# One layer of a hybrid encoder: small steps and small tiles moved at the start, at the first scores and at the end

## The chip, the cores and the metric

The kernel runs on one core of a Trainium2 chip. The metric is the device time of one execution in microseconds (us); where several runs of a kernel are known, their median stands for it.

A core has a matrix engine (TensorE, PE in the profile; the load of its weights has a line of its own, PEld), three engines for elementwise work (VectorE = DVE, ScalarE = ACT, GpSimd = POOL), and SyncE (SP), which in this kernel only issues DMA transfers. Each engine runs its own instructions in the order in which the program issues them, and waits on semaphores for the others. Tiles lie in SBUF (128 partitions wide); results of TensorE lie in PSUM banks of 128 x 512 float32.

## What is computed

One layer on x of 256 tokens by 2048 features, in float32:

```
h = rmsnorm(x) * g1
q, k, v, u = split(h @ w_in)           # 12 query heads, 4 key and value heads of 128; u has 512 columns
a = rmsnorm(window_attention(q, k, v)) # |t - s| <= 128, a slope per head on |t - s|, a sink logit per head
f = rmsnorm(per group of 128 channels: real(fft2(u)) @ w_fourier)
x = x + concat(a, f) @ w_out
h = rmsnorm(x) * g2
gate, val = split(h @ w_up)            # 5504 columns each
x = x + (gelu(conv3(gate)) * val) @ w_down
y = rmsnorm(x) * gf
```

An rmsnorm multiplies each token's row by (mean of its squares + 1e-6)^-0.5, one scale per token, and by a gain per feature. Because the scale belongs to a token, it can be applied behind a matrix product; the kernel does so.

## The kernel before

**Units.** All weights together are some 180 MB, and every weight is used once. They come as units of 128 x 2048 float32 (1 MB): 0 to 3 for u, 4 to 7 for v, 8 to 23 for the query and key heads in the order k0, q0, q1, q2, k1, ..., 24 to 39 for w_out, and then the feed-forward part. TensorE multiplies float32 in a shortened form, so each operand is cut in two: `hi`, a cast copy, and `lo`, the rest. A unit is loaded by a DMA issued on SP into one of three `raw` buffers (L121), ACT makes `hi` from it (L143), DVE makes `lo` = raw - hi (L144), and the load of unit i + 3 is issued right behind the split of unit i (L146), since it takes that unit's buffer. The product is hi x hi + hi x lo + lo x hi. For u, v, w_out and w_down the weights are the moving operand, 512 columns wide, three matmuls for each block of 128 features and each half of the tokens (`moving_weights`, L269 to L271). For q, k and w_up the weights stand still (`still_weights`, L280 and L281).

**The order of steps.** Nothing is scheduled by a planner: the order on each engine is that of the code. `unit(i, work)` (L312) does, for every unit from 4 on up to the end of w_out: the steps hung `before` i, the matmuls of unit i, the steps hung `beside` i, then `step(i)`, which splits unit i + 2, then the steps hung `behind` i. A step hung on a unit puts its matmuls ahead of that unit's on TensorE, or its copies ahead of the split of unit i + 2 (beside) or behind it (behind) on ACT, DVE and POOL. Within one list, the order is that of registration.

**The start.** SP issues the pieces of the transposed input xT (`load_x`; eight tiles of 256 KB, the first in two halves) and of units 0, 1 (quarters) and 2 (halves) in an order written out by hand (L175 to L198). For each of the 16 feature blocks k, `split_scaled` (L230) makes the parts of x times g1, ACT and DVE split a piece of the weights, and six matmuls add to the two u banks `ps_u` (loop at L324). At k = 0 the first piece of the weights is split ahead of the scaled x; at other k behind it.

**Scales of the tokens.** The untransposed x comes as four tiles `xs` of 128 x 2 x 512, issued after the loads of units 4 and 5 (L202 to L207). `token_sums(c)` (L352) takes two sums of squares on ACT for a tile; `token_scales` (L356) adds them up on DVE, raises to the power -0.5 on POOL, copies the result to `r1` on DVE and derives three small tiles for the scores from it. The sums of tiles 0 and 1 stand behind unit 4, those of 2 and 3 and the scales behind unit 5. With `r1`, `rows_out` (L365) cuts u into `u_hi` and `u_lo` beside unit 6, and v beside unit 8.

**The Fourier part.** A small product of the channel matrix with w_fourier (`fourier_weights`, ahead of unit 6) is copied out beside unit 6, and so is the split of the position matrix, `pos_hi` on ACT and `pos_lo` on DVE (`fourier_positions`, L421). Ahead of unit 7, `fourier_rows` multiplies u by the positions (24 matmuls into four `ps_f`, L449). Ahead of units 8 and 9 stand two channel groups each (`fourier_channels`, L468), and beside them `fourier_channels_out` (L473): a copy on ACT, three joins on DVE, the split into a `cat` tile and a square on ACT and DVE, and an addition of squares on POOL (L402). The sum of the squares over the features, `ps_totf`, stands ahead of unit 11. `spread` (L251) turns `r1` from a column into a row across all partitions, with two diagonals on DVE, two matmuls and a copy, all ahead of unit 8.

**The scores.** q and k heads leave PSUM beside the unit behind theirs (`qk_out`, `qk_parts`); the scores of a head stand ahead of the second unit behind its own, that is those of q0 (unit 9) ahead of unit 11. ACT's last step before them is `qT` (L232).

**The end.** The last group of w_down is computed block by block, (column block c, token half b) in the order (0,0), (0,1), (1,0), (1,1), (2,0), (3,0), (2,1), (3,1), the last in two halves p of 256 columns. `last_post` (L808) adds a block to `xs` on DVE (L811), takes its sum of squares on ACT (L797) and multiplies it by the last gain on POOL, unless c is 3 (L814). `finish(b, n)` (L818) adds up n sums, makes the scale (DVE L240, POOL L242) and writes the four outputs y of a token half: two on ACT (L833), one on DVE with two inputs (L827), one on DVE with one (L831). `finish(0, 4)` stands at (3,0), ahead of the additions of block (2,1); `finish(1, 5)` comes last.

**Pools.** `base` holds what lives throughout, `ph` (named "pa") what lives to the end of w_out, `wp` the raw, hi and lo buffers; `wp`'s addresses follow those of `base`.

The functions that the change touches, and their callers:

Of the kernel before, what the change touches and what calls it, by code (L numbers as in the profile page):

```python
# [20 lines left out]
GQA = 3  # L21
NG = 4
AW = NH * HD
FW = NG * P
DFF = 5504
NF = DFF // P
EPS = 1e-6
# [29 lines left out]
def block_kernel(  # L57
# [17 lines left out]
    nc = tc.nc  # L75
# [10 lines left out]
    def bank(pool, name):  # L86
        return pool.tile([P, 512], F32, tag=pool.name, name=name)
# [79 lines left out]
    def load_x(c, o=0, n=512):  # L167
        nc.sync.dma_start(xTc[c][:, o : o + n], xT[:, c * 512 + o : c * 512 + o + n])
# [6 lines left out]
    first = load(0, 4)  # L175
# [4 lines left out]
    next(first)  # L180
    load_x(1)
    next(first)
    load_x(2)
    next(first)
    load_x(3)
    second = load(1, 4)
    next(second)
    load_x(4)
    next(second)
    next(second)  # L190
    load_x(5)
    next(second)
    for _ in second:
        pass
    load_x(6)
    for _ in load(2, 2):
        pass
    load_x(7)  # L198

    def load_more(i):  # L200

# [25 lines left out]
    def vcol(o, n=1):  # L227
        return vec[:, o : o + n]
# [5 lines left out]
            dst[:, S : 2 * S], src, g, f32(dst[:, 0:S]), ALU.mult, ALU.subtract  # L234
        )

    def rstd_of(ssq, width, name, n=2):

        var = base.tile([P, n], F32, tag="var" + name, name="var" + name)
        nc.vector.tensor_scalar(var, ssq, 1.0 / width, EPS, ALU.mult, ALU.add)  # L240
        r = base.tile([P, n], F32, tag="rstd" + name, name="rstd" + name)
        nc.gpsimd.tensor_tensor(r, var, half_pow[:, 0:n], ALU.pow)  # L242
        return r

# [3 lines left out]
            junk, t[:, b, :], AF.Square, accum_out=parts[:, b, c : c + 1]  # L248
        )

    def spread(r, dst, name):  # L251

        ps = bank(dn, "ps_spread" + name)
        for b in range(2):
            dg = base.tile([P, P], F32, tag=f"diag{b}", name=f"diag{name}{b}")
            nc.vector.tensor_scalar(dg, ident, r[:, b : b + 1], None, ALU.mult)
            nc.tensor.matmul(
                ps[:, b * P : (b + 1) * P], ones, dg, start=True, stop=True
            )
        nc.vector.tensor_copy(dst, ps[:, :S])  # L260


    def moving_weights(hi, lo, n, kk, act, b, ps, first, last, q0=0):
# [41 lines left out]
    def at(when, i, f, *a):  # L305
        when.setdefault(i, []).append((f, a))
# [17 lines left out]
    for k in range(NK):  # L324
        c, q = k // 4, k % 4
        if q == 0:
            parts = split_parts(c, 4 if c < 2 else 2)
        if k == 0:
            next(parts)
        split_scaled(hk(k), xTc[k // 2][:, (k % 2) * S : (k % 2 + 1) * S], vcol(V_G1 + k))  # L330
        if k:
            next(parts, None)
        hi, lo = halves[c]
        for b in range(2):
            moving_weights(
                hi, lo, 512, [k], hk, b, ps_u[b], k == 0, k == NK - 1, q0=q
            )
        if q == 3:
            for _ in parts:
                pass  # L340
            del halves[c]
# [1 line left out]
    split(5)  # L343

    ssq1 = base.tile([P, 2, 4], F32, tag="ssq1", name="ssq1")
    r1 = base.tile([P, 2], F32, tag="r1", name="r1")
    rq_neg = base.tile([P, 2], F32, tag="rq_neg", name="rq_neg")
    rq_pos = base.tile([P, 2], F32, tag="rq_pos", name="rq_pos")
    rq_inv = base.tile([P, 2], F32, tag="rq_inv", name="rq_inv")
    sink_neg = base.tile([P, NH], F32, tag="sink_neg", name="sink_neg")  # L350

    def token_sums(c):  # L352
        for b in range(2):
# [38 lines left out]
    def feature_out(ps, slot, g, sq, first):  # L392

        t = cat_pool.tile([P, 512], F32R, tag="cat", name=f"cat{slot}")
        split_scaled(t, ps, g)
        cat[slot] = t
        if first:
            nc.scalar.activation(sq, ps, AF.Square)
        else:
            one = ph.tile([P, S], F32, tag="sq1", name=f"sq{slot}", bufs=1)  # L400
            nc.scalar.activation(one, ps, AF.Square)
            nc.gpsimd.tensor_tensor(sq, sq, one, ALU.add)  # L402
# [67 lines left out]
                us[g][:, o : o + n], start=True, stop=True,  # L470
            )

    def fourier_channels_out(g):  # L473
        h = ph.tile([P, S], F32, tag="tmp", name=f"yh{g}", bufs=2)
        nc.scalar.activation(h, held.pop(("y", g))[:, 0:S], AF.Copy)
        y = ph.tile([P, S], F32, tag="add", name=f"y{g}", bufs=2)
        nc.vector.tensor_tensor(y[:, 1:H], h[:, 1:H], h[:, H + 1 : S], ALU.add)
        nc.vector.tensor_tensor(
            y[:, H + 1 : S], h[:, H - 1 : 0 : -1], h[:, S - 1 : H : -1], ALU.subtract
        )  # L480
        nc.vector.tensor_copy(y[:, 0 : H + 1 : H], h[:, 0 : H + 1 : H])
        feature_out(y, NH + g, vcol(V_GF + g), sq_f, g == 0)

    def token_scales_across():
        spread(r1, r1b, "1")

    def distances():

# [2 lines left out]
            nc.vector.tensor_scalar(rel[:, s], rel[:, s], rq_inv[:, b : b + 1], None, ALU.mult)  # L491
        nc.vector.tensor_scalar(sink_neg, vcol(V_SINK, NH), -1.0, None, ALU.mult)

    at(before, 6, fourier_weights)
# [12 lines left out]


    ps_v = [bank(mm, f"ps_v{b}") for b in range(2)]
# [124 lines left out]
    for i in range(N_QK, N_OUT + 8):  # L634
# [18 lines left out]
        if 2 in heads:  # L653
            at(beside, i, scores_out, heads[2])
            at(behind, i, exps, heads[2])

    for n, (kind, h) in enumerate(QK_ORDER):

        def work(hi, lo):
            ps = st["ps", kind, h] = bank(mm, f"ps_{kind}{h}")  # L660
            still_weights(hi, lo, ps, range(NK))

        unit(N_QK + n, work)
# [151 lines left out]
                xb, xb, gfb[:, c * 512 + o : c * 512 + o + n], ALU.mult  # L815
            )

    def finish(b, n):  # L818
        tot = base.tile([P, 1], F32, tag=f"tot3{b}", name=f"tot3{b}")
        nc.vector.tensor_reduce(tot, ssq3[:, b, 0:n], mybir.AxisListType.X, ALU.add)  # L820
        r = rstd_of(tot, D, f"3{b}", 1)
        y = [
            fp.tile([P, 512], F32, tag="act", name=f"y{b}{c}", bufs=12) for c in range(4)
        ]
        for c in (0, 3, 1, 2):
            if c == 3:
                nc.vector.scalar_tensor_tensor(  # L827
                    y[c], xs[c][:, b, :], r, gfb[:, 1536:2048], ALU.mult, ALU.mult
                )
            elif c == 2:  # L830
                nc.vector.tensor_scalar(y[c], xs[c][:, b, :], r, None, ALU.mult)  # L831
            else:
                nc.scalar.activation(y[c], xs[c][:, b, :], AF.Copy, scale=r)  # L833
            nc.sync.dma_start(
                out[b * P : (b + 1) * P, c * 512 : (c + 1) * 512], y[c]
            )
# [164 lines left out]
```

## Time and profile before

| | us |
|---|---|
| runs | 998.82, 999.02, 1000.75; median 999.02 |
| profiled execution | 999.48 |
| its span (first to last instruction) | 997.6 |
| TensorE busy | 982.8 (99%) |
| VectorE busy | 696.9 (70%) |
| ScalarE busy | 466.6 (47%) |
| GpSimd busy | 23.5 (2%) |
| DMA, mean over the span | 187 GB/s |

The profile has several views. The first page's head gives the busy time of each engine. *Busy time by stretch* gives, for a window A:B in us from the span's start, its length, then the busy time of PE, PEld, DVE, ACT and POOL with their counts, the clock granted to TensorE, and the mean busy share of the 16 DMA engines with the GB/s. *The timeline* gives a start, a duration, the engine, the line, the operation, the tile written and those read, and in brackets the idle time of the engine before it with what ended it. *TensorE's waits* gives, for a tile and the producer waited for, the total, the count and the longest. *The chain of waits* is the chain of work that ended last, in order of time: start, duration, engine, tile and line. Matmuls are pipelined: a row's duration goes from its start to its end, and the next one can start before.

### The profile page before, as it was taken

Reading aid. Unit: us, or ns where it says so; the run is one execution under the profiler, and the core shown is the slowest. Engines: PE = TensorE matmul, PEld = TensorE weight load, DVE = VectorE, ACT = ScalarE, POOL = GpSimd, SP = SyncE. Lnnn points to the kernel's source line nnn. Section 1 sums busy time; section 2 is a strip of 40 time slices with the busy share of each in tenths; the row PEclk is TensorE's granted clock in tenths of the full one; section 3 lists DMA queues with packets and bytes.
Section 4 is the critical chain, followed back from the end, with each engine's and each line's share of the span. In section 5 each row is a group of like instructions: output and inputs, shape, how many; then the busy total and the mean of one; then the engine's idle time right before and its main releaser. Section 6 shows DMA issues by size and latency. Waiting matters only on the chain.

```text
span 997.6 us, 12850 instructions
## 1 busy us (share of the span) xinstructions
PE 982.8 (99%) x5185; PEld 839.6 (84%) x5185; DVE 696.9 (70%) x934; ACT 466.6 (47%) x587; POOL 23.5 (2%) x35
## 2 busy tenths in 40 slices
PE   8999999999999999999999999999999999999996
PEld 6788888888888888888888888888888888888885
DVE  6567877666687776767767767767676777676764
ACT  6646666554554434444434434344344343443434
POOL 0000000000000000000000000000000000000003
PEclk9999999999999999999999999999999999999998
DMA  9834434445645555555555555555645555555532
GB/s 335 339 127 169 165 132 169 135 169 208 239 156 191 187 193 193 188 194 187 174 206 171 210 172 201 177 193 185 209 170 195 185 180 200 173 205 188 194 127 85
DMA packets 30091, 186.42 MB, mean 187 GB/s; under 512 B 3408, under 2 KB 3920, under 8 KB 9040
## 3 DMA queue, kind: packets, MB, share of 16 engines
q1 hardware_dynamic: 29744, 184.54, 52.5%
q8 instruction: 41, 0.67, 0.3%
q0 software_dynamic: 144, 1.05, 0.3%
q14 instruction: 18, 0.15, 0.0%
q10 hardware_dynamic: 144, 0.01, 0.0%
HBM read 183.49 MB, written 2.10 MB: 186 GB/s over the span
## 4 chain that ended last, share of the span: by engine, by line
PE 92%; DMA 3%; ACT 2%; DVE 2%; issue 0%; SPq 0%; POOL 0%; ACTq 0%; POOLq 0%
PE ps_val L280 16%; PE ps_gate L280 16%; PE ps_gate L281 8%; PE ps_val L281 8%; PE ps_d L269 7%; PE ps_d L271 7%; PE ps_d L270 7%; PE ps_q L280 4%; DMA raw<-in_w_in 3%; PE ps_a L271 2%; PE ps_a L269 2%; PE ps_a L270 2%; PE ps_q L281 2%; PE ps_k L280 1%; ACT hi L143 1%; PE ps_s L549 1%
## 5 line engine op out<-in xcount | busy, mean ns | idle before, releaser
L144 DVE TENSOR_TENSOR lo<-raw,hi 128x2048 fp32r<-128x2048 f32 (+3 forms) x178 | 388.5, 2183 | 101.0 <-ACT hi L143 101.0
L143 ACT ACTIVATE hi<-raw 128x2048 fp32r<-128x2048 f32 (+3 forms) x177 | 324.3, 1832 | 171.3 <-PE ps_d L270 106.0
L280 PE MATMUL ps_val<-hU,hi 128*128 128x512 f32 x688 | 245.1, 398 | 0.0
L280 PE MATMUL ps_gate<-hU,hi 128*128 128x512 f32 x688 | 245.1, 397 | 0.0
L281 PE MATMUL ps_gate<-hU,lo 128*128 128x256 f32 x688 | 193.3, 281 | 0.0
L281 PE MATMUL ps_val<-hU,lo 128*128 128x256 f32 x688 | 193.3, 281 | 0.0
L280 PEld LDWEIGHTS ps_val<-hU,hi 128*128 128x128 f32 x688 | 129.3, 188 | 31.9
L280 PEld LDWEIGHTS ps_gate<-hU,hi 128*128 128x128 f32 x688 | 129.3, 188 | 31.8
L281 PEld LDWEIGHTS ps_gate<-hU,lo 128*128 128x128 f32 x688 | 129.1, 188 | 0.4
L281 PEld LDWEIGHTS ps_val<-hU,lo 128*128 128x128 f32 x688 | 129.2, 188 | 0.0
L269 PE MATMUL ps_d<-hi,act 128*128 128x512 f32 x320 | 124.6, 389 | 0.0
L271 PE MATMUL ps_d<-lo,act 128*128 128x512 f32 x320 | 124.6, 389 | 0.0
L270 PE MATMUL ps_d<-hi,act 128*128 128x512 f32 x320 | 124.5, 389 | 0.0
L758 ACT ACTIVATE ft_g<-ps_gate 128x256 f32<-128x256 f32 x43 | 16.5, 383 | 135.1 <-PE ps_gate L281 135.1
L805 DVE TENSOR_TENSOR xs<-ps_d,xs 128x512 f32<-128x512 f32 x80 | 54.6, 688 | 25.6 <-PE ps_d L271 25.6
L271 PEld LDWEIGHTS ps_d<-lo,act 128*128 128x128 f32 x320 | 60.1, 188 | 12.6
L269 PEld LDWEIGHTS ps_d<-hi,act 128*128 128x128 f32 x320 | 60.1, 188 | 12.6
L270 PEld LDWEIGHTS ps_d<-hi,act 128*128 128x128 f32 x320 | 60.1, 188 | 12.2
L280 PE MATMUL ps_q<-hT,hi 128*128 128x512 f32 x192 | 68.6, 399 | 0.0
L758 ACT ACTIVATE ft_v<-ps_val 128x256 f32<-128x256 f32 x43 | 16.5, 383 | 99.5 <-PE ps_val L281 99.5
L760 DVE TENSOR_TENSOR fa_g<-ps_gate,ft_g 128x256 f32<-128x256 f32 x43 | 18.3, 425 | 56.2 <-ACT ft_g L758 56.2
L281 PE MATMUL ps_q<-hT,lo 128*128 128x256 f32 x192 | 54.0, 281 | 0.0
(174 smaller groups left out, 1035.5 us busy)
## 6 DMA issues: line engine op xcount, KB each, us to landing
raw<-in_w_up SPq DMA_DIRECT2D x86, 1024.0 KB, 4.8
raw<-in_w_down SPq DMA_DIRECT2D x40, 1024.0 KB, 4.8
raw<-in_w_in SPq DMA_DIRECT2D x21, 1024.0 KB, 4.9
raw<-in_w_out SPq DMA_DIRECT2D x16, 1024.0 KB, 4.8
raw<-in_w_down_last SPq DMA_DIRECT2D x4, 768.0 KB, 4.2
raw<-in_w_in SPq DMA_DIRECT2D x8, 256.0 KB, 6.4
xs<-in_x SPq DMA_DIRECT2D x4, 512.0 KB, 10.4
out_y<-y SPq DMA_DIRECT2D x8, 256.0 KB, 2.6
```

The costliest lines, as they stand in the source:

```text
L143: nc.scalar.activation(hi[:, s], raw[:, s], AF.Copy)
L144: nc.vector.tensor_tensor(lo[:, s], raw[:, s], f32(hi[:, s]), ALU.subtract)
L269: nc.tensor.matmul(ps, ah, wh, start=first and q == q0, stop=False)
L270: nc.tensor.matmul(ps, al, wh, start=False, stop=False)
L271: nc.tensor.matmul(ps, ah, wl, start=False, stop=last and q == q0 + len(kk) - 1)
L280: nc.tensor.matmul(ps, hi[:, s], h, start=k == 0, stop=False)
L281: nc.tensor.matmul(ps[:, 0:S], lo[:, s], h[:, 0:S], start=False, stop=k == NK - 1)
L549: nc.tensor.matmul(ps[:, b * S : (b + 1) * S], qT[:, qo + b * P : qo + (b + 1) * P], kT[:, ko : ko + S], start=n == 0, stop=n == 2,)
L758: nc.scalar.activation(tmp, ps[:, S : 2 * S], AF.Copy)
L760: nc.vector.tensor_tensor(add, ps[:, 0:S], tmp, ALU.add)
L805: nc.vector.tensor_tensor(xb, ps[b], xb, ALU.add)
```

## The change

- **First loads.** The hand-written order of SP's transfers at the start changes. With `w1.0` for the first piece of unit 1, before: x0a, w0.0, x0b, w0.1, x1, w0.2, x2, w0.3, x3, w1.0, x4, w1.1, w1.2, x5, w1.3, x6, w2.0, w2.1, x7. After: x0a, w0.0, x0b, w0.1, x1, w0.2, w0.3, x2, w1.0, w1.1, x3, w1.2, w1.3, x4, w2.0, x5, w2.1, x6, x7. In the loop, block k = 0 now takes the scaled x ahead of the first piece of the weights, as the other blocks do.
- **Token sums, r1 and the u rows.** All eight sums and the scales stand beside unit 4, ahead of the split of unit 6. POOL writes `r1` itself, with no copy. The three small tiles for the scores are made behind unit 5 (`query_scales`). The u rows and the positions' split move from beside unit 6 to beside unit 5.
- **Spread.** `spread` becomes two functions; for r1 the diagonals are made behind unit 6, the matmuls stay ahead of unit 8, and the copy to `r1b` stands beside unit 8, behind the v rows.
- **Fourier channels.** One channel group for each of units 8 to 11 in place of two for 8 and 9: matmuls ahead of unit i, copy beside i, joins behind i, the rest (`feature_out`) beside i + 1. They are registered behind the steps of the attention heads. The sum of the squares goes from unit 11 to unit 14.
- **The end.** `finish` is cut in three. For token half 0 the scale is made at (3,0), but the four outputs come behind the additions of block (2,1). For token half 1 the reduction over four sums and the step "times 1/D plus epsilon" (`most_of`) are made between the two halves of the last block, and `last_scale` adds the fifth sum and raises to the power, behind the last addition. DVE has one instruction more.
- **Pools.** `rq_neg`, `rq_pos`, `rq_inv` and `sink_neg` go from `base` to `ph`; `r1` and `rstd1` become one tile; two small tiles `part3` are new. With this the raw, hi and lo buffers lie 128 bytes lower.

```diff
-    load_x(2)
     next(first)
-    load_x(3)
+    next(first)
+    load_x(2)
     second = load(1, 4)
...
-        if k == 0:
-            next(parts)
         split_scaled(hk(k), ...)
-        if k:
-            next(parts, None)
+        next(parts, None)
...
-    rq_neg = base.tile(...)            # and rq_pos, rq_inv, sink_neg
+    rq_neg = ph.tile(...)
...
-        r = rstd_of(tot1, D, "1")
-        nc.vector.tensor_copy(r1, r)
+        rstd_of(tot1, D, "1", r=r1)
+
+    def query_scales():
         nc.vector.tensor_scalar(rq_neg, r1, -(HD**-0.5), None, ALU.mult)
...
-    at(behind, 4, token_sums, 0)
-    at(behind, 4, token_sums, 1)
-    at(behind, 5, token_sums, 2)
-    at(behind, 5, token_sums, 3)
-    at(behind, 5, token_scales)
-    at(beside, 6, rows_out, u_hi, u_lo, ps_u)
+    for c in range(4):
+        at(beside, 4, token_sums, c)
+    at(beside, 4, token_scales)
+    at(beside, 5, rows_out, u_hi, u_lo, ps_u)
+    at(behind, 5, query_scales)
...
+    at(beside, 5, fourier_positions)
     at(before, 6, fourier_weights)
     at(beside, 6, fourier_weights_out)
-    at(beside, 6, fourier_positions)
+    at(behind, 6, lambda: spread1.update(d=spread_diagonals(r1, "1")))
...
+    at(before, 8, lambda: spread1.update(ps=spread_sums(spread1["d"], "1")))
     at(beside, 8, lambda: rows_out(v_hi, v_lo, ps_v))
-    for g in range(NG):
-        at(before, 8 + g // 2, fourier_channels, g)
-        at(beside, 8 + g // 2, fourier_channels_out, g)
-    at(before, 8, token_scales_across)
+    at(beside, 8, lambda: nc.vector.tensor_copy(r1b, spread1["ps"][:, :S]))
     at(behind, 8, distances)
-    at(before, 11, total, sq_f, "f")
-    at(beside, 11, total_scale, "f", FW)
+    def fourier_channels_steps():          # called behind the attention steps
+        for g in range(NG):
+            i = 8 + g
+            at(before, i, fourier_channels, g)
+            at(beside, i, fourier_channels_copy, g)
+            at(behind, i, fourier_channels_join, g)
+            at(beside, i + 1, fourier_channels_out, g)
+        at(before, 14, total, sq_f, "f")
+        at(beside, 14, total_scale, "f", FW)
...
         if (c, b) == (3, 0):
-            finish(0, 4)
+            r3 = last_scale(0, 3, most_of(0, 3))
+        if (c, b) == (2, 1):
+            finish(0, r3)
     for p in range(2):
...
         last_post(3, 1, ps[:, 0:256], p * 256, 256, 3 + p)
-    finish(1, 5)
+        if p == 0:
+            var = most_of(1, 4)
+    finish(1, last_scale(1, 4, var))
```

The two new functions at the end:

```python
def most_of(b, n):
    nc.vector.tensor_reduce(tot, ssq3[:, b, 0:n], X, ALU.add)
    nc.vector.tensor_scalar(var, tot, 1.0 / D, EPS, ALU.mult, ALU.add)

def last_scale(b, n, var):
    nc.vector.scalar_tensor_tensor(v, ssq3[:, b, n : n + 1], 1.0 / D, var, ALU.mult, ALU.add)
    nc.gpsimd.tensor_tensor(r, v, half_pow[:, 0:1], ALU.pow)
```

More of the change, by code (lines that the diff above doesn't have):

```diff
@@ L182, in block_kernel @@
     next(first)
+    next(first)
     load_x(2)
-    next(first)
-    load_x(3)
     second = load(1, 4)
     next(second)
-    load_x(4)
+    next(second)
+    load_x(3)
     next(second)
     next(second)
-    load_x(5)
-    next(second)
+    load_x(4)
     for _ in second:
         pass
+    third = load(2, 2)
+    next(third)
+    load_x(5)
+    next(third)
     load_x(6)
-    for _ in load(2, 2):
+    load_x(7)
+    for _ in third:
         pass
-    load_x(7)
     def load_more(i):
@@ L235, in split_scaled, with rstd_of @@
         )
-    def rstd_of(ssq, width, name, n=2):
+    def rstd_of(ssq, width, name, n=2, r=None):
         var = base.tile([P, n], F32, tag="var" + name, name="var" + name)
         nc.vector.tensor_scalar(var, ssq, 1.0 / width, EPS, ALU.mult, ALU.add)
-        r = base.tile([P, n], F32, tag="rstd" + name, name="rstd" + name)
+        if r is None:
+            r = base.tile([P, n], F32, tag="rstd" + name, name="rstd" + name)
         nc.gpsimd.tensor_tensor(r, var, half_pow[:, 0:n], ALU.pow)
@@ L249, in row_ssq, with spread_diagonals @@
         )
-    def spread(r, dst, name):
-        ps = bank(dn, "ps_spread" + name)
+    def spread_diagonals(r, name):
+        dgs = []
         for b in range(2):
@@ L256, in spread, with spread_sums @@
             nc.vector.tensor_scalar(dg, ident, r[:, b : b + 1], None, ALU.mult)
+            dgs.append(dg)
+        return dgs
+    def spread_sums(dgs, name):
+        ps = bank(dn, "ps_spread" + name)
+        for b in range(2):
             nc.tensor.matmul(
-                ps[:, b * P : (b + 1) * P], ones, dg, start=True, stop=True
+                ps[:, b * P : (b + 1) * P], ones, dgs[b], start=True, stop=True
             )
-        nc.vector.tensor_copy(dst, ps[:, :S])
+        return ps
+    def spread(r, dst, name):
+        nc.vector.tensor_copy(dst, spread_sums(spread_diagonals(r, name), name)[:, :S])
     def moving_weights(hi, lo, n, kk, act, b, ps, first, last, q0=0):
@@ L345, in block_kernel @@
     ssq1 = base.tile([P, 2, 4], F32, tag="ssq1", name="ssq1")
[L346 to L350, printed above, removed]
+    r1 = base.tile([P, 2], F32, tag="rstd1", name="rstd1")
+    rq_neg = ph.tile([P, 2], F32, tag="rq_neg", name="rq_neg")
+    rq_pos = ph.tile([P, 2], F32, tag="rq_pos", name="rq_pos")
+    rq_inv = ph.tile([P, 2], F32, tag="rq_inv", name="rq_inv")
+    sink_neg = ph.tile([P, NH], F32, tag="sink_neg", name="sink_neg")
     def token_sums(c):
@@ L481, in fourier_channels_out @@
         nc.vector.tensor_copy(y[:, 0 : H + 1 : H], h[:, 0 : H + 1 : H])
-        feature_out(y, NH + g, vcol(V_GF + g), sq_f, g == 0)
-    def token_scales_across():
-        spread(r1, r1b, "1")
+    def fourier_channels_out(g):
+        feature_out(held.pop(("y", g)), NH + g, vcol(V_GF + g), sq_f, g == 0)
     def distances():
@@ L816, in last_post, with finish @@
             )
-    def finish(b, n):
+    def most_of(b, n):
         tot = base.tile([P, 1], F32, tag=f"tot3{b}", name=f"tot3{b}")
         nc.vector.tensor_reduce(tot, ssq3[:, b, 0:n], mybir.AxisListType.X, ALU.add)
-        r = rstd_of(tot, D, f"3{b}", 1)
+        var = base.tile([P, 1], F32, tag=f"part3{b}", name=f"part3{b}")
+        nc.vector.tensor_scalar(var, tot, 1.0 / D, EPS, ALU.mult, ALU.add)
+        return var
+    def last_scale(b, n, var):
+        v = base.tile([P, 1], F32, tag=f"var3{b}", name=f"var3{b}")
+        nc.vector.scalar_tensor_tensor(
+            v, ssq3[:, b, n : n + 1], 1.0 / D, var, ALU.mult, ALU.add
+        )
+        r = base.tile([P, 1], F32, tag=f"rstd3{b}", name=f"rstd3{b}")
+        nc.gpsimd.tensor_tensor(r, v, half_pow[:, 0:1], ALU.pow)
+        return r
+    def finish(b, r):
         y = [
```

10 lines of the change are left out of this document (7 added, 3 removed).

## Prediction

> **What bounds the kernel now.** I read the page first, then busy time by stretch, TensorE's own waits, and the timeline of all engines where TensorE waits.
>
> ```profile
> span 997.6 us, 12850 instructions
> PE 982.8 (99%) x5185; PEld 839.6 (84%) x5185; DVE 696.9 (70%) x934; ACT 466.6 (47%) x587; POOL 23.5 (2%) x35
> ```
>
> ```profile
> 0.00:12.00 12.00, 9.51 (x40) 7.05 (x40) 4.83 (x10) 5.70 (x10) 0.88 (x8) 1.00 0.80 260
> 100.00:200.00 100.00, 100.00 (x595) 88.39 (x594) 73.78 (x156) 62.63 (x118) 7.77 (x11) 1.00 0.44 151
> 980.00:998.00 18.00, 8.39 (x46) 7.13 (x44) 7.52 (x16) 7.31 (x18) 6.16 (x6) 0.79 0.32 117
> ```
>
> ```profile
> PE ps_s L549 <- ACT qT L232: 1.4, 1, 1.4
> PE ps_f L449 <- ACT pos_hi L422: 0.9, 1, 0.9
> ```
>
> TensorE is idle 997.6 - 982.8 = 14.8 us, most of it at the start and after its last matmul; from 100 us it runs full. The change touches only places with such idle time: the first loads, two waits before 80 us, the end. So a microsecond saved on TensorE before 100 us comes off the end, since everything behind it moves along, and nothing else counts.
>
> **The change, part by part.**
>
> **First loads and the first step.**
>
> ```profile
> 12.07 0.63 ACT L143 ACTIVATE hi<-raw 128x512 fp32r<-128x512 f32 x1 [0.29 <-DMA raw<-in_w_in]
> 17.35 1.06 ACT L143 ACTIVATE hi<-raw 128x1024 fp32r<-128x1024 f32 x1 [0.92 <-DMA raw<-in_w_in]
> 19.72 0.50 PE L271 MATMUL ps_u<-lo,hT 128*128 128x512 f32 x1 [0.39 <-DVE lo L144]
> 30.36 0.39 PE L269 MATMUL ps_v<-hi,hT 128*128 128x512 f32 x1
> ```
>
> ```profile
> 13.48 8.33 DMA raw<-in_w_in
> 23.01 1.23 DVE lo L144
> ```
>
> No DMA is added on SP's queue; they change places. The first quarter of unit 1 (split at 12.07) and the first half of unit 2 (17.35) both begin as their data lands, with eight pieces of 256 KB between: (17.35 - 12.07)/8 = 0.66 us a piece. In the new order two pieces (xT 5 and 6) no longer stand ahead of that half: 1.3 us earlier. The matmul at 19.72 waited for its lo part, so it gains 1.3 us. But unit 3 (the DMA issued at 13.48, landing 21.8) keeps the same bytes ahead of it. Its first lo half ends at 23.01 + 1.23 = 24.24 as before. Matmuls follow each other by 0.229 us (21 steps from 43.54 to 48.34, rows below), so the one that needs this half ran at 19.72 + 24 x 0.229 = 25.2; it can come 0.9 us earlier, no more. The u product ends 0.9 us earlier, at 29.45. The scaled x of step 0, now ahead of the cast on DVE, only fills a gap there: the loads behind it decide. Ends: 0 (lateness in landing eats it) to 1.3.
>
> **Token sums and r1 a unit earlier** (eight sums on ACT now ahead of unit 6's split, not shared out behind units 6 and 7).
>
> ```profile
> 30.73 1.92 ACT L143 ACTIVATE hi<-raw 128x2048 fp32r<-128x2048 f32 x1 [3.80 <-DMA raw<-in_w_in]
> 35.96 1.92 ACT L143 ACTIVATE hi<-raw 128x2048 fp32r<-128x2048 f32 x1 [3.31 <-DMA raw<-in_w_in]
> 37.78 0.61 ACT L247 ACTIVATE junka<-xs 128x512 f32<-128x512 f32 x1
> 40.66 1.89 ACT L143 ACTIVATE hi<-raw 128x2048 fp32r<-128x2048 f32 x1
> 37.91 2.29 DVE L144 TENSOR_TENSOR lo<-raw,hi 128x2048 fp32r<-128x2048 f32 x1 [2.94 <-ACT hi L143]
> 43.54 0.39 PE L271 MATMUL ps_v<-lo,hT 128*128 128x512 f32 x1
> ```
>
> Four sums take 40.66 - 37.78 = 2.88. Unit 5's split (30.73, held by its DMA) frees ACT 37.78 - 35.96 = 1.82 later, at 32.55; eight sums (5.8 to 5.9) put unit 6's split at 38.4 instead of 35.96; its lo starts 37.91 - 35.96 = 1.95 later and ends at 40.35 + 2.29 = 42.64. TensorE wants that at 43.54 - 0.9 = 42.64: no slack left. I take 0.05 for the hand-over: gain up to here 0.85. The xs loads stand ahead of unit 6's on SP, so they landed before 35.9 at the latest; then the last four sums put the split at 38.8 and cost 0.4 more. Behind it, unit 9's load waits for this lo, 2.4 us later than before; its use is 20 us off. The copy of r1 on DVE (L360) goes, off any wait.
>
> **Positions beside unit 5.**
>
> ```profile
> 48.34 0.40 PE L271 MATMUL ps_v<-lo,hT 128*128 128x512 f32 x1
> 53.25 0.39 PE L269 MATMUL ps_v<-hi,hT 128*128 128x512 f32 x1
> ```
>
> ```profile
> 86.68 0.71 PE ps_s L549 x6
> 208.94 0.34 PE ps_tota L409 x4
> ```
>
> Six matmuls of 256 columns take 0.71 (scores, in the chain of waits), so the 24 of ps_f need 2.84 us behind 48.34 + 0.23 = 48.57; the next stage would start at 51.41, not 53.25: 1.84 us lost to pos_hi, pos_lo and the restart. In the new order ACT does the u rows at about 40.3, pos_hi at 41.6, then unit 7's split; DVE does u_lo and pos_lo by about 44.8 and unit 7's lo by 47.1. TensorE asks for the first at 47.7 and the last at 51: the whole 1.84 goes. Lower end: the listed wait alone, 0.9.
>
> **Fourier channels spread over units 8 to 11**, each join, copy and output apart.
>
> ```profile
> 74.78 1.90 ACT L143 ACTIVATE hi<-raw 128x2048 fp32r<-128x2048 f32 x1
> 77.93 0.50 PE L409 MATMUL ps_totf<-ones,sq_f 128*128 128x1 f32 x4
> 80.88 0.39 PE L280 MATMUL ps_q<-hT,hi 128*128 128x512 f32 x1
> ```
>
> Four channel outputs now hold up ACT and DVE until 74.78, so the first qT is late. Without that, totals (0.34) and scores (0.71) would end at 78.98; they end at 80.88: 1.90 lost. In the new order: unit 8 starts near 57.1 (unit 7 at 50.6, 24 steps of 0.229, and 1 us for the spread's and the first channel's matmuls) and takes 5.7 (80.88 to the scores at 86.68 is 5.8); ACT clears v_hi and one copy by 57.4, unit 10's split by 59.3; DVE its lo by 61.6, distances and one join by 62.9; then k's outputs, one channel, unit 11's split and lo by 69.8, a join, add_q 70.9, qT 71.8. TensorE asks for it at 74.9: 3.1 us of slack, and some 2 to 3.4 us for the next two heads. The spread's diagonals, made at about 50, cost its matmuls no wait; the totals move to unit 14 at the same price. Lower end: the listed 1.4.
>
> **The end: last additions first.**
>
> ```profile
> 985.85 0.39 PE L271 MATMUL ps_e<-lo,act 128*128 128x512 f32 x1
> 986.78 1.34 ACT L833 ACTIVATE y<-xs,rstd 128x512 f32<-128x512 f32 x2 [1.04 <-POOL rstd L242]
> 989.38 0.42 ACT L797 ACTIVATE junkc<-xs 128x256 f32<-128x256 f32 x1
> 989.92 0.42 ACT L797 ACTIVATE junkc<-xs 128x256 f32<-128x256 f32 x1
> 991.48 0.75 DVE L827 SCALAR_TENSOR_TENSOR y<-xs,rstd,gfb 128x512 f32<-128x512 f32 x1 [0.67 <-POOL rstd L242]
> ```
>
> ```profile
> 984.24 0.70 DVE xs L811
> 985.02 0.73 ACT junkc L797 x2
> 985.78 0.17 DVE tot L820
> 985.97 0.17 DVE var L240
> 986.20 0.56 POOL rstd L242
> 989.43 1.26 POOL xs L814
> ```
>
> Times here are those of before. The addition of block (2,1) starts at 985.85 + 0.39 + 0.04 = 986.28, not behind the outputs. Its square starts 985.02 - 984.24 = 0.78 later and takes 0.73: 987.79. The two outputs on ACT (1.34) now follow it: 989.1. The square of the first half takes 989.92 - 989.38 = 0.54: 989.64. Now the new wait: most_of stands on DVE between the two last additions and waits for that square; its two steps (0.19 each, 985.78 to 985.97) hold the last addition until 990.0. Addition 0.42, square 0.54, last_scale 0.2, rstd 0.56 and hand-overs give the scale at 991.8, against 991.48: 0.3 us worse. Ends: 0 and 1.4 worse (the rival below).
>
> **Sum.** 0.85 + 1.84 + 1.90 - 0.3 = 4.3 us. The profiled execution took 999.48 (1.9 around its span), 0.46 above the median of 999.02; so 995.2 for it, 994.8 against the median.
>
> **The rivals.** *GpSimd holds DVE at the end.*
>
> ```profile
> 71.22 0.74 POOL L402 TENSOR_TENSOR sq_f<-sq_f,sq 128x256 f32<-128x256 f32 x1 [5.32 <-ACT sq L401]
> 71.44 0.66 DVE L477 TENSOR_TENSOR y<-yh 128x127 f32<-128x127 f32 x1
> 72.03 0.28 DVE L478 TENSOR_TENSOR y<-yh 128x127 f32<-128x127 f32 x1
> ```
>
> Beside a GpSimd instruction that had begun, a DVE one of 0.28 took 0.66 and ended just after it. The new order puts GpSimd's scaling of block (2,1) (1.26 at 989.43 before) at about 987.86, and DVE's output of one input at 986.28 + 0.70 + 0.75 = 987.7. DVE is first by 0.13; if it is second it waits until 989.1 and the scale comes some 1.1 us later: 995.9. The Trainium skill ("SBUF — State Buffer", Who interferes with whom) says that whichever of a DVE operation in a two-port mode and a GpSimd operation starts first keeps the shared port pair to its end; by that rule the collision is real, and the trace agrees for the two-input case (0.66 beside 0.28). Chance 0.1.
>
> *A new wait replaces one of the two* (unit 6's lo, or a qT in units 11 to 13, whose ACT and DVE now carry the channel outputs): against it stands the slack above. One of 1.9 us back: 996.7. Chance 0.12.
>
> *Loads land better than in strict turn*, so the head's 1.3 and no wait at unit 6: 994.3. Chance 0.08.
>
> *Nothing changes*: TensorE's stalls only move, as 0.9 moved to unit 6. Against it: from 100 us there is no other stall to find. 999. Chance 0.07.
>
> *Slower: addresses.* Each small tile takes a multiple of 32 bytes; five go and two come, so every weight tile lies 128 bytes lower, and the attention tiles change by 32 modulo 64. If that lengthened matmuls by 4.3/982.8 = 0.44% (0.8 ns of each), the gain is gone; at 1%, 9.8 us, 1004.6. The trace has only one layout and cannot exclude it; the relative places of raw, hi and lo stay. Chance 0.11.
>
> **How the numbers follow.** My forecast has 0.52. Faster by over 0.2% (2 us, about what a measurement here can tell): it, the two cases near it and most of the replaced wait, 0.81; within 0.2%: 0.08; slower: 0.11. The low end takes all ends at once, 1.3 + 1.84 + 1.90 = 5.0, and 0.3 for the median: 993.7. The high end is the replaced wait and the collision in part: 997.5. That leaves out no change and slower.
>
> **What would show it.** Right: no wait of ps_f on pos_hi nor of ps_s on qT in TensorE's list; the first ps_v near 29.5; the third matmul of unit 6 near 42.7, the q product that ran at 80.88 near 76; the last scale 0.3 us later behind the last matmul than before; matmul means unchanged. Wrong: a wait of ps_v on lo above 0.5 us, one of ps_s or ps_t before 100 us, or longer matmuls.

## The result, and the profile after

The changed kernel takes 990.69 us (median of 4 runs, 989.97 to 991.63), the kernel before 999.46 over the 4 runs then known: a ratio of 0.9911, with a 95% interval of [0.9894, 0.9928]. The forecast was 994.8, between 993.7 and 997.5: the direction held, but the gain is 8.8 us where 4.2 were forecast (against the 999.02 known then), and the time lies below the range.

The page of the changed kernel, and the list of what TensorE waited for, answer to the lines shown of before. (In the list: tile, line, the producer waited for, then total, count and longest in us.)

```profile
span 988.2 us, 12858 instructions
PE 977.0 (99%) x5185; PEld 838.2 (85%) x5185; DVE 696.1 (70%) x935; ACT 466.5 (47%) x587; POOL 23.6 (2%) x35
```

```profile
PE ps_warm L228 <- POOL ones L220: 1.0, 1, 1.0
PE ps_u L282 <- ACT hi L143: 0.9, 2, 0.6
```

The waits of `ps_f` (the u rows times the positions) on `pos_hi` and of `ps_s` (scores) on `qT` are gone, as forecast. But TensorE's busy time fell too, from 982.8 to 977.0, with the same 5185 matmuls. A removed stall takes idle time away, 14.8 - 11.2 = 3.6 us here; the other 5.8 us came out of time in which TensorE counts as busy. The forecast had no such term.

Where it came from is read by the starts of the first matmul of each stage. The timeline of before (30.36 and 53.25, the first v product and unit 7, stand in the prediction), then that of after:

```profile
171.84 0.40 PE L269 MATMUL ps_a<-hi,cat 128*128 128x512 f32 x1
266.45 0.39 PE L280 MATMUL ps_gate<-hU,hi 128*128 128x512 f32 x1
971.80 0.39 PE L269 MATMUL ps_e<-hi,act 128*128 128x512 f32 x1
```

```profile
29.41 0.39 PE L282 MATMUL ps_v<-hi,hT 128*128 128x512 f32 x1
50.78 0.39 PE L282 MATMUL ps_v<-hi,hT 128*128 128x512 f32 x1
167.28 0.39 PE L282 MATMUL ps_a<-hi,cat 128*128 128x512 f32 x1
261.90 0.40 PE L293 MATMUL ps_gate<-hU,hi 128*128 128x512 f32 x1
962.27 0.39 PE L282 MATMUL ps_e<-hi,act 128*128 128x512 f32 x1
```

| stretch | before | after | gain | forecast |
|---|---|---|---|---|
| start to the first v product (unit 4) | 30.36 | 29.41 | 0.95 | 0.85 |
| to unit 7 | 22.89 | 21.37 | 1.52 | 1.84 |
| to w_out | 118.59 | 116.50 | 2.09 | 1.90 |
| to the first gate | 94.61 | 94.62 | 0 | 0 |
| gates, values, down products to the last group | 705.35 | 700.37 | **4.98** | 0 |
| last group to the end of the span | 25.8 | 25.9 | -0.1 | -0.3 |

Times are in us. The first three rows and the last sum to 4.5, and the forecast's sum was 4.3. The fifth row is new, and it lies in a stretch in which neither kernel has a wait. There, a gate or value unit (16 pairs of matmuls, one with the hi and one with the lo part of the weights) takes a steady time, which two starts in a row show. Before:

```profile
447.00 0.39 PE L280 MATMUL ps_gate<-hU,hi 128*128 128x512 f32 x1
452.65 0.40 PE L280 MATMUL ps_val<-hU,hi 128*128 128x512 f32 x1
```

After, once ahead of the first down products and once behind them:

```profile
285.77 0.40 PE L293 MATMUL ps_gate<-hU,hi 128*128 128x512 f32 x1
291.42 0.39 PE L293 MATMUL ps_val<-hU,hi 128*128 128x512 f32 x1
441.83 0.40 PE L293 MATMUL ps_gate<-hU,hi 128*128 128x512 f32 x1
447.42 0.39 PE L293 MATMUL ps_val<-hU,hi 128*128 128x512 f32 x1
```

A unit takes 5.65 us before. After, it takes 5.65 ahead of the first down products, and behind them 5.59 for the first unit of a group and 5.58 for the others. The 70 units behind them, at 0.07, make the 4.9 us. The change does not touch these matmuls. What it does touch is where their operands lie: hi and lo are 128 bytes lower, while hT (and hU, which takes its place) stays at byte 34,912 of each partition in both kernels.

### The profile page after: what moved, and what is told of

It is laid out like the page before. It is cut to its first block, busy times and chain, and to the rows that moved or that the text cites. A ratio compares the mean times of both kernels' runs of the same rounds, so it can differ in the third digit from the quotient of the medians.

```text
span 988.2 us, 12858 instructions
## 1 busy us (share of the span) xinstructions
PE 977.0 (99%) x5185; PEld 838.2 (85%) x5185; DVE 696.1 (70%) x935; ACT 466.5 (47%) x587; POOL 23.6 (2%) x35
## 4 chain that ended last, share of the span: by engine, by line
PE 98%; DMA 1%; issue 0%; SPq 0%; ACT 0%; POOL 0%; DVE 0%; ACTq 0%; POOLq 0%
PE ps_gate L293 16%; PE ps_val L293 16%; PE ps_val L294 8%; PE ps_gate L294 8%; PE ps_d L284 7%; PE ps_d L283 7%; PE ps_d L282 7%; PE ps_q L293 5%; PE ps_q L294 2%; PE ps_a L284 2%; PE ps_a L282 2%; PE ps_a L283 2%; PE ps_k L293 2%; PE ps_o L642 1%; PE ps_s L570 1%; PE ps_k L294 1%
## 5 line engine op out<-in xcount | busy, mean ns | idle before, releaser
L293 PE MATMUL ps_gate<-hU,hi 128*128 128x512 f32 x688 | 242.6, 394 | 0.0
L293 PE MATMUL ps_val<-hU,hi 128*128 128x512 f32 x688 | 242.6, 394 | 0.0
```

The source lines that it names most:

```text
L293: nc.tensor.matmul(ps, hi[:, s], h, start=k == 0, stop=False)
```

## Experiments

### Placement or steps

```diff
 # kernel before, e1_place: placement of the changed kernel, nothing else
-    rq_neg = base.tile(...)          # and rq_pos, rq_inv, sink_neg
+    rq_neg = ph.tile(...)
...
+    pad = base.tile([P, 8], F32, tag="pad", name="pad")      # unused, cleared once
 # changed kernel, e2_plus128: the weights back at their old addresses
+    pad = base.tile([P, 32], F32, tag="pad", name="pad")
+    nc.gpsimd.memset(pad, 0.0)
     ssq1 = base.tile(...)
```

> The kernel before with the placement of the changed one and nothing else: the four small tiles rq_neg, rq_pos, rq_inv and sink_neg in the pool pa, one unused tile of 32 bytes in base, so raw, hi, lo and the feed-forward tiles lie 128 bytes lower and the attention tiles 32 higher, as in the changed kernel; all steps in the old order. Theory P (the placement of the weights sets the pace of the gate and value products): from the second feed-forward group on behind the first down products a gate or value unit takes 5.59 us in place of 5.65, and the time is about 4.9 us below before (994.6 against 999.5). Theory T (the steps moved, and with them the moment or the state in which the products begin): units stay at 5.65 and the time stays at that of before. Theory B (other PSUM banks of the down products, which this kernel has as before): as T.

> The changed kernel with one unused tile of 128 bytes in base: raw, hi and lo back at the addresses of before (69,536 for the first), PSUM banks and steps as in the changed kernel. P: gate and value units at 5.65 again, time about 4.9 us above the changed kernel (995.5), still 4.5 below before from the stalls that went. T and B: units at 5.59 behind the first down products, time as the changed kernel, 990.5.

Measured: the placement alone 994.53 (993.12 to 996.4), ratio to before 0.9951 [0.9935, 0.9967]; the steps alone, with the old placement, 995.44 (995.12 to 996.63), ratio 0.9958 [0.9941, 0.9975]. Busy time by stretch for 400 to 600 us shows the pace as the number of matmuls in 200 us (the count behind PE's busy time). Before, after, the placement alone, the steps alone:

```profile
400.00:600.00 200.00, 200.00 (x1052) 171.02 (x1051) 142.01 (x166) 83.81 (x84) 0.00 (x0) 1.00 0.53 187
```

```profile
400.00:600.00 200.00, 200.00 (x1061) 171.96 (x1060) 143.35 (x169) 84.69 (x86) 0.00 (x0) 1.00 0.55 191
```

```profile
400.00:600.00 200.00, 200.00 (x1062) 171.97 (x1061) 143.55 (x169) 84.23 (x84) 0.00 (x0) 1.00 0.54 190
```

```profile
400.00:600.00 200.00, 200.00 (x1053) 171.03 (x1052) 142.64 (x168) 84.12 (x84) 0.00 (x0) 1.00 0.54 190
```

1052, 1061, 1062, 1053 matmuls at the same granted clock of 1.00: the pace goes with the placement, both ways, and not with the steps or the PSUM banks of the down products (these banks are as before in the first kernel, as after in the second). So the change is two changes: 4.9 us of placement, and 4 us of steps. The forecast had summed 4.3 for the steps; not all of its terms hold one by one, as the runs below show.

### Which distance

All four are the changed kernel with one unused tile.

```diff
 # p32, p64, p256 (p224 below): 32, 64, 256 bytes ahead of the weights
+    pad = base.tile([P, 8], F32, tag="pad", name="pad")        # 8, 16, 64 columns
+    nc.gpsimd.memset(pad, 0.0)
     ssq1 = base.tile(...)
 # e9_others: behind raw, hi, lo and junk
+    for n in ("junk", "pad"):
+        t = wp.tile([P, 512 if n == "junk" else 32], F32, tag=n, name=n + "0")
+        nc.gpsimd.memset(t, 0.0)
```

> The changed kernel with one unused tile of 32 bytes in base: every weight tile 32 bytes higher (raw0 at 69,440, a multiple of 64, where before and the changed kernel have 32 modulo 64). P1 (only the place modulo 256 that the changed kernel has is fast): units behind the first down products at 5.65, time 995.5. P2 (a distance from the place of before is what counts, any other place is fast): 5.59, 990.7. P3 (a multiple of 64 is better still): under 5.59, and under 989 if the units ahead of the first down products gain too.

> The same with 64 bytes: raw0 at 69,472, halfway between the changed kernel (69,408) and before (69,536). P1: 5.65, 995.5. P2: 5.59, 990.7. If the pace follows the place in steps of 64: between 5.59 and 5.65.

> The same with 256 bytes: raw0 at 69,664, the same place modulo 256 as in the changed kernel, another modulo 512. P256 (the place modulo 256 decides): 5.59 and 990.7. P512 (modulo 512): 5.65 and 995.5.

> The changed kernel with an unused tile of 128 bytes behind the weight tiles: raw, hi and lo stay where the changed kernel has them; the outputs of the gates and values, the activations and the last gain lie 128 bytes higher, where before has them. W (the place of hi and lo, which TensorE reads in these units, decides): 5.59 and 990.7. O (the place of the other tiles, which DVE and ACT write beside it, decides): 5.65 and 995.5.

Measured (one time each, in the order of the four expectations): 987.29, 995.22, 990.73 and 1003.53. A shift of 256 leaves time and pace as they were (5.65 and then 5.59 a unit). 32 bytes more is better than the changed kernel, and 64 as slow as before. The last was the surprise: with hi and lo untouched and only the other tiles moved by 128, it is 3.4 us slower than *before* (1000.17 on the same chip). Its groups by line and the down products of before (on the page, line L269):

```profile
L282 PE MATMUL ps_d<-hi,act 128*128 128x512 f32 x96 | 37.9, 395 | 0.0
```

```profile
L269 PE MATMUL ps_d<-hi,act 128*128 128x512 f32 x320 | 124.6, 389 | 0.0
```

The down products, whose other operand is `act`, take 395 ns each in place of 389; a group of them lasts 22.4 us in place of 21.8, and w_out's products, with `cat` as the other operand, take 96.49 us in place of 94.62. In all other kernels here act moves with hi, and the down products keep their pace. Neither theory W nor O had that. A third fits: what counts is the distance between the two operands of a matmul. (For the down products this rests on the one kernel, in which all tiles behind the weights moved.) For hT it was tested by moving hT along with the weights, and a further distance was taken:

```diff
 # r32_both: 32 bytes ahead of hT instead of behind it
+    pad = base.tile([P, 8], F32, tag="pad", name="pad")
+    nc.gpsimd.memset(pad, 0.0)
     for c in range(4):
         t = base.tile([P, 4, 512], F32R, tag=f"hT{c}", name=f"hT{c}")
```

> The changed kernel with the 32 unused bytes ahead of hT in place of behind it: raw, hi and lo lie at the same addresses as in the kernel with 32 bytes more (raw0 at 69,440), but hT moves along, so that the distance between the two operands of the q, k, gate and value products stays that of the changed kernel. A (the address of the weights by itself decides): 5.55 us for every gate and value unit, about 987. R (the distance of the two operands modulo 256 decides): 5.65 ahead of the first down products and 5.59 behind them, about 990.7.

> The changed kernel with 224 bytes more ahead of the weights: hi lies 160 past hT modulo 256 (192 in the changed kernel, 224 with 32 bytes more, 0 with 64, 64 before). If the fast region lies between 160 and 224: 5.55 to 5.59 for a gate unit, 986 to 991. If 192 is its edge: 5.65, 995.5.

> The changed kernel with 32 bytes more ahead of the weights, timed. Its products of q, k, gates and values go at 0.347 us a pair: at a head no worse than that of the changed kernel's runs 4.2 us under it, since its first product of the last group came 2.74 us earlier than in the changed kernel's profile, although its v products began 2.37 later. 986.5, between 985 and 988.

The kernel with hT moved along has the weights at the very addresses of the fastest kernel (32 bytes more); apart from the unused tile, only hT and hU lie elsewhere. But it took 991.65, with units of 5.65 and then 5.59, as the changed kernel:

```profile
400.00:600.00 200.00, 200.00 (x1061) 171.97 (x1060) 143.50 (x170) 84.86 (x86) 0.00 (x0) 1.00 0.54 190
```

The distance decides; theory A falls. With 224 bytes: 993.08, with 5.60 for each unit. The kernel with 32 bytes more, timed: 985.76 (985.59 to 987.38), ratio to before 0.9859 [0.9845, 0.9874]. It beats both kernels. Its stretch, and two starts in a row (5.56 or 5.57 for the first unit of a group behind down products; 5.55 for the others):

```profile
400.00:600.00 200.00, 200.00 (x1067) 173.41 (x1066) 143.82 (x170) 84.21 (x84) 0.00 (x0) 1.00 0.54 190
```

```profile
439.82 0.40 PE L293 MATMUL ps_gate<-hU,hi 128*128 128x512 f32 x1
445.38 0.39 PE L293 MATMUL ps_val<-hU,hi 128*128 128x512 f32 x1
```

| kernels | hi less hT, modulo 256 | a gate or value unit, us |
|---|---|---|
| 64 bytes more | 0 | 5.65 |
| before, steps alone | 64 | 5.65 |
| 224 bytes more | 160 | 5.60 |
| changed, placement alone, 256 bytes more, 32 ahead of hT | 192 | 5.65, then 5.59 behind the first down products |
| 32 bytes more | 224 | 5.55 |

lo lies at the same place modulo 256 as hi. hT was moved in one of these kernels; in the others the weights moved, and with them what lies behind. At 192 a gate or value unit has two paces, and keeps the one that it has for a whole group of eight. In the kernel whose down products are slow (e9_others, also at 192) it stays at 5.65 behind them as well:

```profile
445.63 0.40 PE L293 MATMUL ps_gate<-hU,hi 128*128 128x512 f32 x1
451.28 0.40 PE L293 MATMUL ps_val<-hU,hi 128*128 128x512 f32 x1
```

So the distance alone does not settle the pace at 192. That what runs ahead of a group picks it is a guess: in e9_others the tiles that ACT and DVE write beside these products had moved too.

### The stalls

```diff
 # e5_old_positions: sums, scales, u rows and positions where before had them
-    at(beside, 5, rows_out, u_hi, u_lo, ps_u)
+    at(beside, 6, rows_out, u_hi, u_lo, ps_u)       # and the other steps likewise
 # e4_old_channels: two channels a unit, copy, joins and output in one step
+        at(before, 8 + g // 2, fourier_channels, g)
+        at(beside, 8 + g // 2, fourier_channels_all, g)
 # e8_chan_spread: e4_old_channels, and
+    at(before, 8, spread, r1, r1b, "1")
 # e10_chan_alone: the kernel before with fourier_channels_steps() of the changed one
```

> The changed kernel with the token sums, the r1 scales, the u rows and the positions where before had them (units 4 and 5 behind, 6 beside). My step sum: ps_f waits for pos_hi and pos_lo again, and the span from the last ps_v ahead of ps_f to the first ps_v behind it grows by 1.8 us; w_out's start about 1.8 later than 167.3 less what the third matmul of unit 6 gains (up to 0.1). Rival (half of that wait is made good by the next units' slack): 0.9 or less.

> The changed kernel with the Fourier channels as before: two for each of units 8 and 9, copy, joins and output together, their total ahead of unit 11, registered ahead of the attention steps. My step sum: the wait of the first ps_s on qT comes back (about 1.4) and the start of w_out's products is 1.5 to 1.9 us later than in the changed kernel (167.3), all else equal. Rival (the wait had another cause, such as the late joining of v rows): no such wait, the start of w_out within 0.3 us of 167.3.

> The changed kernel with the old Fourier channels and the old spread (diagonals, matmuls and the copy of r1b all ahead of unit 8). From the first v product of unit 7 to the first product of w_out the changed kernel takes 116.5 us, with the old channels alone 117.1, before at the old placement 118.6. S (the spread kept DVE from the first qT): 118.3. T (the steps in units 4 to 6 moved the work that made qT late): 117.1 to 117.3.

> The kernel before with the new Fourier channels (one a unit, 8 to 11, total ahead of unit 14) and nothing else. My step sum, in which the channels make the first qT late: no wait of ps_s on qT, the stretch from unit 7's first product to w_out's 116.7 in place of 118.6, time 1.9 below before (997.5). If the channels are worth only 0.6: 118.0, and a wait of ps_s of 0.8 or so is left.

With the old positions (993.41), the stretch from the first v product to unit 7 takes 54.13 - 30.70 = 23.43 in place of 21.37, 2.1 us more, and TensorE's list has the old waits again:

```profile
PE ps_f L461 <- ACT pos_hi L434: 1.2, 1, 1.2
PE ps_f L461 <- DVE pos_lo L435: 0.3, 1, 0.3
```

In this profile the step is worth what was forecast (1.84), but that is one execution. The two other kernels with the old positions, the placement alone and the new channels alone (below), need 52.12 - 29.89 = 22.23 and 52.31 - 30.61 = 21.70 for the same stretch. Neither has the wait on pos_hi. With the new channels alone, ACT's split of unit 5 and `pos_hi`, the last v product ahead of ps_f, and the one wait of ps_f:

```profile
29.80 1.92 ACT L143 ACTIVATE hi<-raw 128x2048 fp32r<-128x2048 f32 x1 [2.71 <-DMA raw<-in_w_in]
48.03 0.65 ACT L422 ACTIVATE pos_hi<-pos 128x512 fp32r<-128x512 f32 x1
48.59 0.40 PE L271 MATMUL ps_v<-lo,hT 128*128 128x512 f32 x1
```

```profile
PE ps_f L449 <- DVE pos_lo L423: 0.3, 1, 0.3
```

In all four profiles with the old positions pos_hi starts 18.0 to 18.3 us behind the split of unit 5, which waits for its DMA. In the kernel before this put it 0.64 us behind the start of the last v product (48.98 against 48.34), here 0.56 ahead of it. With the placement alone it is 0.34 ahead, with the old positions in the changed kernel 0.87 behind, and the stretch grows in the same order: 21.70, 22.23, 22.89, 23.43. So the price of the old positions depends on when that load lands against the start of the v products: 0.3 to 2.1 us over the 21.37 of the changed kernel, 1.2 in the mean of the four.

The channels are not so simple. The stretch is now from unit 7 to w_out. One line of TensorE's list for the kernel with the old channels, and one for that with the old channels and the old spread:

```profile
PE ps_s L571 <- ACT qT L235: 0.3, 1, 0.3
```

```profile
PE ps_s L569 <- ACT qT L235: 1.4, 1, 1.4
```

The old channels alone (991.92) cost 169.20 - 52.12 = 117.08, only 0.58 above the changed kernel; with the old spread too (993.27) it is 170.55 - 52.12 = 118.43, and the whole stall is back. Yet the new channels alone, in the kernel before (996.64), need 169.09 - 52.31 = 116.78, 1.81 less than before, with no wait of ps_s. So both parts unload DVE and ACT ahead of the first qT: the channels alone remove the whole stall, the spread alone 1.34 of it, and together they leave slack. A stall can be removed in full by either of two parts, and undoing one shows only what the other doesn't cover.

### First loads

```diff
 # e3_old_loads: changed kernel, order of the first loads and the step k = 0 as before
```

> The changed kernel once more, beside the two below on the same chip: 990.7, within 0.5. Its start of the v products (29.4 us in its first profile) is between 29.4 and 31.8, as in the other kernels with the new order of the first loads, if what lands first is a matter of chance from one execution to the next.

> The changed kernel with the order of the first loads, and the first step of the loop, as before. My step sum: 0.85 us slower than the changed kernel (991.5 against 990.7), v products later by 0.9. Rival (the landing of the first pieces varies by more than their order moves them: starts of 29.4 to 31.8 with the new order, 29.9 and 30.4 with the old): within 0.4 of the changed kernel, either way.

On the same chip: the changed kernel 991.15 (990.8 to 992.18), with the old loads 990.84 (990.66 to 991.41). The new order brings no gain that can be seen. The first v product shows why. The changed kernel's second profile, the old loads, and the latest of the new order (224 bytes more):

```profile
31.57 0.40 PE L282 MATMUL ps_v<-hi,hT 128*128 128x512 f32 x1
```

```profile
30.19 0.40 PE L279 MATMUL ps_v<-hi,hT 128*128 128x512 f32 x1
```

```profile
32.02 0.40 PE L282 MATMUL ps_v<-hi,hT 128*128 128x512 f32 x1
```

The same kernel began its v products at 29.41 and at 31.57. Over 14 profiles with the new order the start lies between 29.41 and 32.02, median 30.72; over 4 with the old between 29.89 and 30.61, median 30.28. One execution differs from the next by more than the 0.85 us that the order was to bring.

### The end

```diff
 # e6_old_end: changed kernel with finish(0, 4) at (3,0) and finish(1, 5) last
```

> The changed kernel with the old end: the four outputs of token half 0 ahead of the additions of block (2,1), all sums and the scale of token half 1 behind the last addition. From the first product of the last group to the end of the span: 25.9 us in the changed kernel, 25.8 before. My step sum had the new end 0.3 worse: 25.6 here. Rival (the new end is better and something else lengthened it): 26.1 or more.

Measured 990.62. From the first product of the last group to the end: 988.85 - 963.03 = 25.82, against 25.92 in the changed kernel. The new end is 0.1 us worse. Its mechanism is in the changed kernel's timeline (DVE and ACT behind the last matmuls):

```profile
978.17 1.32 ACT L869 ACTIVATE y<-xs,rstd 128x512 f32<-128x512 f32 x2
979.39 0.40 ACT L819 ACTIVATE junkc<-xs 128x256 f32<-128x256 f32 x1
979.92 0.16 DVE L843 TENSOR_REDUCE tot<-ssq 128x1 f32<-128x4 f32 x1 [1.09 <-ACT junkc L819]
980.18 0.41 DVE L833 TENSOR_TENSOR xs<-ps_e,xs 128x256 f32<-128x256 f32 x1
982.06 0.75 DVE L863 SCALAR_TENSOR_TENSOR y<-xs,rstd,gfb 128x512 f32<-128x512 f32 x1 [0.67 <-POOL rstd L854]
```

ACT's outputs of half 0 (978.17) delay its square of the first half (979.39); the reduction on DVE waits 1.09 us for that square, and the last addition (980.18) stands behind it.

## Why the prediction was wrong

**The step that failed**: the sum has no term for the pace of the matmuls. It says that the change "touches only places with such idle time" and that "nothing else counts", and the 705 us of gates, values and down products stand in it at nothing. The runs show 4.98 us there, and the placement alone brings them (705.35 to 700.38). The one place where the prediction looks at it is the rival *Slower: addresses*. It named the right fact ("every weight tile lies 128 bytes lower") and the right stage, the matmuls. It then took a change of pace for a loss only (chance 0.11) and closed with "the relative places of raw, hi and lo stay". These do, but hi and lo meet hT in TensorE, and hT did not move. The bound was one-sided: it weighed 0.44% and 1% of TensorE's time as a loss, and the runs show 4.98/705.35 = 0.7% of the stretch as a gain. Taken to both sides, the same 0.44% would have put the low end near 990. The page of before held a hint, easier to see afterwards, that the pace was not the best. Matmuls of the same shape, 512 columns, have a mean of 389 ns among the down products (above) and 397 among the gates:

```profile
L280 PE MATMUL ps_gate<-hU,hi 128*128 128x512 f32 x688 | 245.1, 397 | 0.0
```

In the changed kernel the gates' mean is 394, so the sign "matmul means unchanged" did not come, and with 32 bytes more it is 390.

**First loads** (0.85 forecast): the matching 0.95 of the first profile is chance; old and new order give 990.84 and 991.15. The step took the landing times of one execution for those of every one.

**Token sums and the third matmul of unit 6**: the forecast had its lo end at 42.64 with no slack. In the changed kernel:

```profile
39.52 2.29 DVE L144 TENSOR_TENSOR lo<-raw,hi 128x2048 fp32r<-128x2048 f32 x1 [1.44 <-ACT hi L143]
42.78 0.39 PE L284 MATMUL ps_v<-lo,hT 128*128 128x512 f32 x1
```

It ends at 41.81, 1.0 ahead of its use: unit 6's split came earlier than reckoned, so the price of 0.05 for the hand-over did not arise.

**Positions** (1.84): the right wait, but its size was that of one execution: 1.52 in the first pair of profiles, 2.1 when undone, and 0.3 and 0.9 against the two other kernels with the old positions. **Channels** (1.90): right in size (1.83 at the old placement, 118.59 - (168.86 - 52.10)), and the sum of the new order held; qT was ready with time to spare, 70.74 + 0.42 against the 71.8 forecast, for a use at 74.92:

```profile
70.74 0.42 ACT L235 ACTIVATE qT<-add_q 128x256 fp32r<-128x256 f32 x1 [1.22 <-DVE add_q L549]
74.92 0.63 PE L570 MATMUL ps_s<-kT,qT 128*128 128x256 f32 x4
```

But the cause was named too narrowly, since the spread alone removes most of it. That the steps came to some 4 us in all is in part luck, since no gain is shown for the first loads and the price of the positions varies. The other 0.26 us of that row goes with the placement (116.76 for the steps alone, 116.50 in the changed kernel).

**The end** (0.3 worse): the wait is the one forecast, at a third of its price.

**The rivals.** *GpSimd holds DVE* did not come: DVE's output of one input started at 978.02, GpSimd's scaling at 978.34. *A new wait* and *nothing changes* did not come either. *Loads land better* can't be told from the spread of the first loads.

## What to carry to other kernels

A change of small tiles is a change of placement. For a kernel that, like this one, is bound by its matmuls, write down where the operands of the main products lie relative to each other (here modulo 256 bytes), before and after, and when one moves against the other allow for a pace that is better or worse by 1 to 2%. Then try a few unused tiles of 32 bytes each: here one of them was worth 5 us more on top of the change, more than all the reordering. Which distance is best in another kernel was not measured. And an effect in the first 30 us read from one execution is no effect until a second one shows it.

## What was not expected of the hardware

In this kernel the pace of TensorE depends on the distance between a matmul's two operands in SBUF, and the one shift by 256 bytes that was run left it as it was. With hT, a unit takes 5.65 us at 0 and 64, 5.60 at 160, 5.55 at 224, and 5.65 or 5.59 at 192. The down products take 389 ns at distance 0 and 395 at 128: distance 0 is the slow one for the first form of product and the faster of the two for the other. Nothing waits in the trace: the matmuls only start a few ns apart from where they did, at a granted clock of 1.00. The Trainium skill ("SBUF — State Buffer", SBUF: two separate sides) says that only the port pair shared by VectorE and GpSimd causes contention among the engines, and that TensorE waits on nobody; that is about engines against one another, and no run here contradicts it: behind 100 us TensorE's list has no wait at either pace. Whether the dependence on the distance comes from SBUF, from the load of the weights or from within TensorE is not shown.
